# One layer of a hybrid token mixer: a mask moved behind a product, a scaling moved to ScalarE, larger VectorE instructions, and a new written-out order

## The chip, the cores and the metric

The kernel runs on one core of one Trainium2 chip. The metric is the device time of one execution in microseconds, here the median of three runs. All work is float32; large products run as three products of two float32r halves.

## The reference

The function is one layer over 512 latent tokens and 256 context tokens, width 1024. What matters here is its first half:

```python
zc = _modulate(_rmsnorm(hc, g_pre1), csh1, csc1) @ w_in     # context, 7584 columns
z  = _modulate(_rmsnorm(h,  g_pre1), sh1,  sc1)  @ w_in     # latent
# RWKV-7 branch, 16 heads of 64, two directions:
def step(s, inp):
    r_t, w_t, k_t, v_t, kk_t, b_t = inp
    s_a = einsum('dbhvk,dbhk->dbhv', s, -kk_t)
    s = s * w_t[..., None, :] + s_a[..., None] * b_t[..., None, :] + v_t[..., None] * k_t[..., None, :]
    return s, einsum('dbhvk,dbhk->dbhv', s, r_t)
# RG-LRU branch: gates, then h = a * h + b over the tokens, two directions
mixed = gates[..., :D] * (y_a @ w_branch_a) + gates[..., D:] * (y_b @ w_branch_b)
h = h + gt1 * _rmsnorm(mixed @ w_out, g_post1)
# then a mixture of 64 experts (top 6) with a shared expert, and a last residual
```

The modulation vectors come from `silu(c) @ w_mod + b_mod`.

## The kernel before

The kernel has three parts in time. First the tokens are normalized, and the first third of the modulation is computed. Then `mixers()` (line 548) runs the input projection and both mixers. Then `moe()` runs the output projection, the router and the experts. The change touches `mixers()` alone, besides one constant.

The mixers work on eight pairs of heads (j, 128 channels each). A pair has three stages g of 256 tokens: one of context and two of latent tokens, so there are 24 stages n = 3j + g. A stage holds both directions d, and in each four chunks i of 64 tokens. The sequential recurrence is turned into products per chunk:

- `s1` (1011) makes the decay and its running product; `s1c` (1049) makes from it the operands AR (key and receptance, scaled) and BK (three slots of 64 columns per chunk; slots 0 and 2 hold the same product k times the inverse decay, slot 0 for the lower and slot 2 for the upper 64 partitions, slot 1 the second key).
- `s1b` (1109, "A-stage") multiplies BK with AR into PSUM and masks the result to its causal half, into AM. Stage 0 of a pair has one such product group, stages 1 and 2 have two. It then transposes BK into BKt.
- `p_sub` (1233) inverts the 16x16 diagonal blocks: AM goes to a DRAM buffer Dg, comes back as L with one block per partition, DVE substitutes, and the result goes back through Qg. In line 1248 POOL then sets AM's entries inside the diagonal blocks to zero, in place, by the constant `offd`.
- `p_mrg` (1298) merges the 16x16 inverses into a 64x64 one: a first product of AM with the block diagonal DD, copied by ACT into NT, and three more steps (`mm`, then an addition on DVE).
- `p_chain` (1341) runs over the chunks. Per chunk: a first product of the state H and of AM with UV into `ch`; a copy X on DVE; a product with Q; copies into UV on DVE (one half) and ACT (the other); a product with BKt; and the new state H = Pc * (product) + HP on DVE, where HP = H * Pc is the old state scaled by the decay Pc, made by POOL (1381). In stages 1 and 2 the output products into `py` follow.

Beside these run `p_in` (675, the input projection, 128 columns at a time, in steps of two of its eight row blocks), `weight_stream` (483, loads a weight half, splits it on ACT and DVE), `p_lru` (746), `p_uv`, `p_kk`, `p_bonus`, `p_post` (1458, the normalization after a pair's chain), `p_br` (859, the branch projections) and `p_mod` (903: the other two thirds of the modulation, 16 rounds of a 1 MB load and 8 products; at its end it stores zeros into the two buffers `y_d` that the experts add into, with sixteen DMAs on SyncE's queue). `p_mod` borrows the buffers of `y` and `kds`, so that stage 1 (n = 1) of `s1c` and of the chain starts after it.

Each of these fifteen is a generator. Between two `yield`s it issues the instructions of one step, mostly for one engine. `Flow.run` (137) walks through the string ORDER: each letter with its number advances one generator so many steps. As PE, DVE, ACT and POOL keep the order in which instructions are issued, this string alone sets each engine's queue. SyncE's DMAs are placed by the same program order. A generator may also yield an event or a lock (PSUM buffers `a` and `b` are shared through locks); these too take one advance.

The instruction on the end of the loop reads:

```python
yield ACT if first else DVE
if first: S.activation(Hn[:, d, :], ch[:, 4 + d, :], AF.Copy, scale=Pc[:, d, i:i + 1])
else:     V.scalar_tensor_tensor(Hn[:, d, :], ch[:, 4 + d, :], Pc[:, d, i:i + 1], HP[:, d, :], op0=ALU.mult, op1=ALU.add)
```

Of the kernel before, what the change touches and what calls it, by code (L numbers as in the profile page):

```python
# [63 lines left out]
PE, DVE, ACT, POOL = "PE", "DVE", "ACT", "POOL"  # L64
ORDER = (
    "idwi2ludri4w2idniwi6ciwsw2iei2widiwiwi3wiwiwi3w2i2wiwi2bwi2ldwi5w3idw2miriwi2ri3r2w2ir2driwrwkwiwiriroirik2i5rik"
    "wldrwi3w3ri2kwkilpkikiluwuilil2irkiwuliulwiliukdwkurlukiuwlire2wie2wieiwei2u2ruiwreuwe2uediwdudweirie2ie2l2idib"
# [3 lines left out]
    "b3r2b4erlb2e2r2se2bererseserebe3s4crs4es6res5e3relb2ibi2rkbir2sbmblwrmwr2lrmklr2mrli2lrlb2mlwnlbimibrnibimlbmrsi"
    "mkmc2b2csrlckckeirc3wi2wkrc2kcscwi2kcs2ws2rsws2rcs2r2s2c2s3c2sciricksrc2kscncsc2skirscinsewcec3ic3wemierme3iwcie"
    "cewc2eicrne2cem2emc2ecmeliliwlmr2wcbcumlimlucwkl3ulmcb2mcuriucwcrb2cbucibc3wscblic3licecicwciebier2eis2ececiece3"
    "bcscw2scs2r2cswurscis4rc2sircs4cscucisc2irsi2cicscsc2iecrwicwc2isce2ciu2eremumu3meucpiewirwup2eiemepwerbwmlrcibl"
    "rl3ml3pmlipl2pb2primbieibrbwmerirwmwmrpcpc2bceieb2wc2bpribwecesic3e2cwilcpeiwiwbeicepcspiwcprecp2crcs3rs4c2sps3c"
    "scs3iwpscisbcsw2c3eicsciwrsc2se2crwcsc3meu2iure2u2e2iuwi2b2ibr2lbkbcrmblir2kr2lcwl2mlriwirl2umb2mnlmlwbmbim2uri"
    "b2rimkmwc2sli2skecnwcbcwbkcricsirc2srsisis3kcri2ckcs5csnskrw2rkcwc2ics3rc2kcsrc2s2crickc2nwsec2sic2icie2c2ece2nw"
    "emecicmiwe3cieceicm2ec2rmcmwcmeimewlulwlumlbiu2lclrwlburlmblbci2mbc2rcb2cuwc2l2urbwukecrc3ecbecic2eciceberece2i"
    "e2s2ri4sc3ec2eswrsrwcscirs2csiscrcws2rs3cs2i2scscsicw2csics2crcsc2mcieiewrc5u2reiuipiru2eurmeieuiurprwpm2e2relbr"
    "lrwrmwlipl2miblprpilbwcblwl3miwemimiebcibm2c2b2ecb2cbibwiececpecp2ececes2ipbcirsepwcew2cwiciricwpec2bpcrcipscs6"  # L80
    "c3ls4pscsipse2sc2swcpsecwpcsic2sicwic2rpecescesrceu2wic2uiu2ebmwrurbwmrbi2bri2bmlbuklwr2irnrlurlwmrl2nilrbrlbmlb"
    "lbkmsibikwisi2m3wb2mrmc5bkisc3srwr2ckcscki2si2sws2csls2icsrsckcrkscscsrkiswscsrcec2kwnwc2scsikec3ensc3wcicrc2e2c"
    "semecie2kciw2mieci2ecmece2cec3memwremui2blmlrwumlrclir2wml2wmnbl2ulirmubrl2c2wec2b2ceuibubc2ecsbcre2cbecscic2ic"
    "i2ci2uececbe2wr2sc3i2e2srs3c3srus2cscrscsecwics3iw2csrisc2scrsc3wscesic3i2ci2cscicueusueuimuepucuweiwue2r2iermr2"
    "eimwpwpilwrlmbmplpr2lrbl2rmpilmli2mblbwicmrlwrib3lmewmec2ecbibecwibpb2cwpcecpeieblpeiceisec2eic2prwc2espwiwcse2c"
    "iwcsc2p2sp2s4c2peps4rs2pcrs2csiwscsc2icisciwes2cwcbwc3sc2e2ci2e2umurmnu2w2ubibrkiuilbr2nurmbkibwmbrwrlwlrl2r2l2u"
    "licrbr2imbrkbmlmlibmbw2biscs2imilmbmcwc3kbkicrciekcrcicrc2is4is2rsiskskw2s2c2rc2sirs2c2sckicnwrscscskc3rscs2ikei"
    "c3ieie4wmcmc2nce2rwe2icic2ec2ecwkie2cmimewc3memlwcicmlcmurlcrblmlrl3bnwirblmumiuc2lblrcbcb2cbwceuce2cir2ecece2uc"
    "eciuwcscic2i2bcieieresecwrbcsecs3ic2rcis2w2crcs2ucsus2icswscsrs2c2siscircsrwsc2ic5ec2sc2uei2rirusuiumueueweiepru"
    "iui2pewrewem2iwbwpmrpbml3mrlml2pr2l2ir2iblpcriribwb3wimibml2we2mbmcec2iwbc2bcscsbe2cipc2epwe2cwi2pcicip2ecespewc"  # L90
    "ecwpc2picricwsps2bscesps2crplpscs5piscs2ircscwc2bwicseisc2wsercicecsc3u3cieuwmue2uelrb2rw2biri2burnbirm2wbilrmwr"
    "lml4ur2krwbl2imb2mbirsrmlbklbikcnmisrmswmwcebwbrc2kci2c3i2crcki2k2c2r2iwscws3ns5csrcscrs3icscksicsrcrkc2kcs3cwi"
    "c2wkeic2nwesikwcecmcicrime2c2iece2rec4iceie3iecwcre2lm2cmc2lmlmblcblrnwlrlurwmbuluiumrmlcmuc3buic2b2clclbcswirw"
    "c3eciec2ibe2i2ecsebicerciwuecsceicbwcere2cwes2rcs2crics2ic2swur2cs2isis3wiscicscscsrisc3scs2cic2meceic3iuruwu2c"
    "u2perermieie2ieu2mwcp2ebrl2iwmrwirmwl2rml3mliwb2rpml3iwebmibp2ibrimbwebmc2ebecbircsbrbpcecpipcwe3src2eipewci2wps"
    "ewc2ecwpcicibcwprc2sipscs3p2csr2pes4pcscs2ilspc2ws2wcswci2csc2s2iec2ecrcse2c2ecuwu2beiumuieiulbnbrmbwrbr2cib2lri"
    "niur2umwrlmlilrmrlrl3wbicmbwkiwrkblblwbmsmbwiwimib2km2c2sc2rckic2rcskr2kci2cs2ikisciscrws2csickes2rcrskcsic2scsi"
    "ks3rsc2wcisrcwsnwcrskc3nsec2i2ec3erecewiecic2e3cecm2ewimcirc2wem2ec2m2eicwe2l2c2bmlr2l2mulinwl2b2ilmlkmwbucwcurb"
    "ucurcbuc2rici2cisbcliebcbecesrceciwescibc2ie2ieuce2wecec2weusrsrsc4rs4cs2crscis3csi2wcs2cscisicrcsrwc5ecs2c2i3e"
    "c2uwmu2ewurueueimimiuipruepewe2prpl2prwliwcbrlprpm2lrlbplmibr2il2rwbpmbrmicilblb2mibimwb2sepewpewribe2wmc2pecewp"  # L100
    "sceceiecpsepe2bces4cisicwcs2rc2ps2iepsps3wscwr2isc2isc2iscpwilwcscsiwscrcsbciecrwceic2icoecec2oemwlkcrkc2bokokrc"
    "k3lrcmcoblmrlu2l2o2lu3bol2ubnbmobo2momncub2mulbobm2bskloem2bnwocsob2cock2cocokcncsce3osc4s2ecoc3scscs2c3scos2csc"
    "ososcs2o2co2escscwscocseo2s2c3ewewewc2oe2ocmo2ncececec2wc2me2l3cw2uwmlml2ouob2lmlcwbmbl2umb2lme2cemomsueoemc2bec"
    "wbe4o2webcucscswocecueceuc2wus3cecsowoes2wc2soc2se3scs2c3ocscsoswcwc2oswsc3oscs2cebwowcoseocesmlmwbwc3l2col4clc2"
    "lc2wco2lbmcwubo2lebu2mu2bwbmobwm2wb2mbeomcem2sc2b2epec3eo2e2ceu2cesucscpoecpcecwcwp2cwop2cs3cp2cebseco2pcwscpws"
# [2212 lines left out]
```

## Time and profile before

| | |
|---|---|
| time, median of 3 runs | 2006.52 us (2000.51 to 2008.1) |
| the profiled execution | 2014.62 us, its span 2012.7 us |
| mean granted TensorE clock | 0.936 |
| PE busy | 1741.5 us (87%) |
| DVE busy | 1095.7 us (54%) |
| ACT busy | 714.3 us (35%) |
| POOL busy | 553.9 us (28%) |
| HBM read, written | 340.72 MB, 56.92 MB |

PE is TensorE's products, DVE is VectorE, ACT is ScalarE, POOL is GpSimd, SP or SPq is SyncE and its queue of DMAs. A line L1248 is line 1248 of the kernel. Times in the rows are microseconds from the start of the span. An engine's idle time is put down to what ended it. The granted clock is a share of TensorE's full 2.4 GHz. The mixers run from about 55 to about 1232 us.

### The profile page before, as it was taken

What the parts mean: (1) busy time and instruction counts of PE and PEld (TensorE: products, weight loads), DVE (VectorE), ACT (ScalarE), POOL (GpSimd) and SP (SyncE); (2) the same over time, 40 slices, a digit from 0 to 9 for tenths busy, and PEclk for the clock granted to TensorE, in tenths of its full rate; (3) what the DMA queues carried; (4) which work ended last, traced back from release to release, by engine and by line L of the source; (5) the groups of instructions that cost most, each with busy time, mean ns of one, the idle gap of its engine ahead of it and who ended that gap; (6) DMA issues with size and microseconds to landing.
All of it is one profiled execution on the core that took longest, in us unless ns stands there. A gap on an engine that the chain in (4) does not pass through costs nothing.

```text
span 2012.7 us, 41091 instructions
## 1 busy us (share of the span) xinstructions
PE 1741.5 (87%) x16550; PEld 1106.0 (55%) x16550; DVE 1095.7 (54%) x2721; ACT 714.3 (35%) x1308; POOL 553.9 (28%) x557
## 2 busy tenths in 40 slices
...
GB/s 278 155 140 158 142 112 59 68 84 56 87 58 73 78 64 82 58 87 63 77 123 114 106 155 250 288 210 303 387 372 306 347 376 387 320 379 396 405 353 130
DMA packets 310267, 386.72 MB, mean 192 GB/s; under 512 B 172390, under 2 KB 252860, under 8 KB 292540
## 3 DMA queue, kind: packets, MB, share of 16 engines
...
HBM read 340.72 MB, written 56.92 MB: 198 GB/s over the span
## 4 chain that ended last, share of the span: by engine, by line
PE 59%; DMA 14%; DVE 13%; issue 7%; ACT 5%; SPq 1%; POOL 1%; DVEq 0%; POOLq 0%; ACTq 0%
PE ps_zl L524 17%; PE mgu L2187 10%; PE my L1690 5%; PE ps_m L1321 4%; PE ps_zc L526 3%; DMA wgu<-in_ex_w_gu 2%; DMA y_d<-ys,ix 2%; DMA DD<-Qg 2%; DMA ug<-u_d,ix 2%; PE ps_a L774 2%; PE ps_a L1126 2%; DMA wdn<-in_ex_w_down 2%; PE ps_z L1572 1%; PE ps_c L1400 1%; PE pt L2180 1%
## 5 line engine op out<-in xcount | busy, mean ns | idle before, releaser
L2187 PE MATMUL mgu<-wgu,uTe 128*32 128x512 f32 (+2 forms) x1488 | 310.8, 614 | 23.5 <-DMA wgu<-in_ex_w_gu 18.4
L524 PE MATMUL ps_zl<-xh,wh 128*128 128x512 f32 (+1 forms) x600 | 267.7, 446 | 6.7 <-DVE xh L452 2.6
L524 PE MATMUL ps_zl<-xl,wh 128*128 128x512 f32 (+1 forms) x600 | 243.2, 405 | 2.7 <-DVE xl L453 1.7
L524 PE MATMUL ps_zl<-xh,wl 128*128 128x512 f32 (+1 forms) x600 | 242.3, 404 | 0.8 <-DVE wl L505 0.8
L2187 PEld LDWEIGHTS mgu<-wgu,uTe 128*32 128x32 f32 (+2 forms) x1488 | 92.1, 129 | 193.6 <-issue 162.0
L2195 POOL DMA_INDIRECT y_d<-ys,ix x65 | 93.3, 1436 | 257.3 <-DVE ys L1693 208.1
L505 DVE TENSOR_TENSOR wl<-wraw,wh 128x512 fp32r<-128x512 f32 (+1 forms) x152 | 112.2, 738 | 83.0 <-ACT wh L502 62.5
L1690 PE MATMUL my<-wdn,hT 128*32 128x512 f32 (+2 forms) x776 | 153.4, 603 | 1.9 <-ACT hT L1686 1.4
L524 PEld LDWEIGHTS ps_zl<-xh,wh 128*128 128x128 f32 (+1 forms) x600 | 114.8, 191 | 51.9 <-issue 10.1
L524 PEld LDWEIGHTS ps_zl<-xh,wl 128*128 128x128 f32 (+1 forms) x600 | 115.6, 193 | 30.7 <-DVE wl L505 2.1
L524 PEld LDWEIGHTS ps_zl<-xl,wh 128*128 128x128 f32 (+1 forms) x600 | 116.3, 194 | 26.7 <-DVE xl L453 3.4
L1381 POOL TENSOR_TENSOR HP<-H,Pc 128x128 f32<-128x128 f32 x88 | 55.2, 627 | 262.8 <-DVE H L1409 210.5
L1693 DVE COPY ys<-my 128x512 f32<-128x512 f32 x41 | 28.3, 691 | 181.3 <-ACT ys L1692 175.4
L502 ACT ACTIVATE wh<-wraw 128x512 fp32r<-128x512 f32 (+1 forms) x152 | 94.6, 622 | 84.3 <-PE ps_zc L526 25.4
L1668 DVE SCALAR_TENSOR_TENSOR th<-th,mgu 128x256 f32<-128x256 f32 x39 | 16.0, 415 | 174.4 <-ACT th L1667 174.4
L1667 ACT ACTIVATE th<-mgu 128x256 f32<-128x256 f32 x39 | 14.7, 383 | 270.2 <-PE mgu L2187 262.1
L1248 POOL TENSOR_TENSOR AM<-AM,offd 64x512 f32<-64x512 f32 x48 | 71.1, 1481 | 115.3 <-DMA Dg<-AM 104.7
...
L1690 PEld LDWEIGHTS my<-wdn,hT 128*32 128x32 f32 (+2 forms) x776 | 49.8, 129 | 90.7 <-issue 72.2
L2180 PE MATMUL pt<-ident,ug 128*128 128x128 f32 x296 | 51.6, 307 | 51.3 <-DMA wdn<-in_ex_w_down 25.4
L1692 ACT ACTIVATE ys<-my 128x512 f32<-128x512 f32 x41 | 24.5, 597 | 179.1 <-PE my L1690 172.2
L1394 ACT ACTIVATE UV<-ps_c 64x128 f32<-64x128 f32 x96 | 25.7, 267 | 163.5 <-DVE UV L1391 163.1
(505 smaller groups left out, 3733.3 us busy)
## 6 DMA issues: line engine op xcount, KB each, us to landing
...
wraw<-in_w_in SPq DMA_DIRECT2D x118, 256.0 KB
...
```

Source lines behind the costliest of these rows:

```text
L502: S.activation(wh[:, :, 0:n], raws[m][:, :, 0:n], AF.Copy)
L505: V.tensor_sub(wl[:, :, 0:n], raws[m][:, :, 0:n], wh[:, :, 0:n])
L524: T.matmul(zl[:n], w[:, kc % 4, 0:n], x[:, kc, LAT], start=a, stop=z)
L526: T.matmul(zc[:n], w[:, kc % 4, 0:n], x[:, kc, 0:CTX], start=a, stop=z)
L774: T.matmul(o, gw[q, 2 * d + g, :], r, start=True, stop=True, tile_position=(64 * h, 64 * h))
L1248: G.tensor_tensor(AM[q, h, :, :, 0:64], AM[q, h, :, :, 0:64], offd[q, None, None, :].to_broadcast([64, 4, 2, 64]), op=ALU.mult)
L1321: T.matmul(pm[q, m, 0:w], lhs(q, m), rhs(q, m), start=True, stop=True, tile_position=(64 * h, 64 * h))
L1381: G.tensor_tensor(HP, H, Pc[:, :, i:i + 1].to_broadcast([128, 2, 64]), op=ALU.mult)
L1690: T.matmul(py[q, hf, :], hT[:, k, q], wd[:, k, 512 * hf:512 * hf + 512], start=k == 0, stop=k == 1, tile_position=(0, q.start))
L2180: T.transpose(pt[:, k, :], ug[:, k:D:KC], ident)
L2187: T.matmul(gu[q], uT[:, k, q], wg[:, k, :], start=k == 0, stop=k == KC - 1, tile_position=(0, q.start))
L2195: G.indirect_dma_start(out=y[:, :], out_offset=bass.IndirectOffsetOnAxis(ap=ix[0:n], axis=0), in_=ys[q, :], in_offset=None, bounds_check=S ...
```

## The change

Five things change, all inside the mixers.

The constant `offd` was 1 where the column lies in a later block of 16 than the row, for AM; it becomes 1 where the row lies in a later block than the column, for the product, whose rows are AM's columns:

```diff
-        V.tensor_tensor(offd, cb, pm, op=ALU.is_gt)
+        V.tensor_scalar(cb, cb, 16.0, None, op0=ALU.add)
+        V.tensor_tensor(offd, pm, cb, op=ALU.is_ge)
```

`p_sub` no longer masks AM on POOL, and `p_mrg` masks the first product as it copies it:

```diff
-                for h in range(2):
-                    q = slice(64 - 64 * h, 128 - 64 * h)
-                    yield POOL
-                    lab(f'relayout:{n//3}.{n%3}')
-                    G.tensor_tensor(AM[q, h, :, :, 0:64], AM[q, h, :, :, 0:64], offd[q, None, None, :].to_broadcast([64, 4, 2, 64]), op=ALU.mult)
...
-                yield ACT
-                L()
-                S.activation(NT[:, :, 0:48], pm, AF.Copy)
+                yield DVE
+                L()
+                V.tensor_tensor(NT[:, :, 0:48], pm, offd[:, None, 0:48].to_broadcast([128, 8, 48]), op=ALU.mult)
```

The scaled state HP is made by ScalarE, one instruction for each direction:

```diff
                     if not first:
-                        yield POOL
-                        L()
                         HP = r2.tile([128, 2, 64], F32, name="HP", bufs=1)
-                        G.tensor_tensor(HP, H, Pc[:, :, i:i + 1].to_broadcast([128, 2, 64]), op=ALU.mult)
+                        for d in range(2):
+                            yield ACT
+                            L()
+                            S.activation(HP[:, d, :], H[:, d, :], AF.Copy, scale=Pc[:, d, i:i + 1])
```

Slots 0 and 2 of BK are written for both directions, all chunks and all partitions by one instruction after the loop over d, and the causal mask of A is applied to both heads by one instruction:

```diff
-                yield DVE
-                L('lora+elem')
-                V.tensor_tensor(BK[0:64, d, :, 0, :], c3(kd[0:64]), c3(Ei[0:64, d, :]), op=ALU.mult)
-                yield DVE
-                L('lora+elem')
-                V.tensor_tensor(BK[64:128, d, :, 2, :], c3(kd[64:128]), c3(Ei[64:128, d, :]), op=ALU.mult)
...
+            yield DVE
+            L('lora+elem')
+            c4 = lambda t: t.rearrange("p d (i t) -> p (d i) t", t=64)[:, :, None, :].to_broadcast([128, 8, 2, 64])
+            V.tensor_tensor(BK.rearrange("p d i s t -> p (d i) s t")[:, :, 0:3:2, :], c4(tha), c4(Ei), op=ALU.mult)
...
-                for h in range(2):
-                    yield DVE
-                    L('A-stage')
-                    V.tensor_tensor(AM[:, h, i0:i0 + per].rearrange("p i d w -> p (i d) w"),
-                                    pa[:, h].rearrange("p i d w -> p (i d) w"),
-                                    mask[:, None, 0:W].to_broadcast([128, per * 2, W]), op=ALU.mult)
+                yield DVE
+                L('A-stage')
+                V.tensor_tensor(AM[:, :, i0:i0 + per].rearrange("p h i d w -> p h (i d) w"),
+                                pa.rearrange("p h i d w -> p h (i d) w"),
+                                mask[:, None, None, 0:W].to_broadcast([128, 2, per * 2, W]), op=ALU.mult)
```

ORDER is a new string throughout: 5000 advances in place of 5072. The letters are c chain, m `p_mrg`, u `p_uv`, b `p_s1b`, s `p_sub`, e `p_s1c`, l `p_s1`, k `p_kk`, r `p_lru`, o `p_br`, d `p_mod`, n `p_bonus`, p `p_post`, i `p_in`, w the weight stream. Its first and its last line:

```diff
-    "idwi2ludri4w2idniwi6ciwsw2iei2widiwiwi3wiwiwi3w2i2wiwi2bwi2ldwi5w3idw2miriwi2ri3r2w2ir2driwrwkwiwiriroirik2i5rik"
...
-    "w2o2p2wowo2pwow2opop2wop2owpwpwpop"
+    "pwlcibormdi3dwidi2ni2dui3w4i4wiwi2wedwi2kwi5wi3w3idi2w2i2sw2i4diw2iwi2widirw2i4r4w2rwidri2r2irliwiwrir2di2k2rkld"
...
+    "cw2owco2c2wc3o2wcwcwoc2o2woc4ocwcwc2wc2o2c2wc3o2cwc2oc2ocop3wp2op2wp3w2p3owp2opop2owp2w2p2o"
```

## Rows read from the trace of the kernel before

**Rows 1.** Windows: busy us and count of each engine, clock, DMA share, GB/s.
```profile
60.00:240.00 180.00, 169.93 (x1249) 118.33 (x1249) 80.58 (x135) 80.59 (x148) 20.12 (x19) 0.97 0.52 151
240.00:295.00 55.00, 29.02 (x161) 20.61 (x159) 43.88 (x69) 23.15 (x33) 22.59 (x21) 0.66 0.42 129
...
60.00:1240.00 1180.00, 1065.42 (x12951) 804.47 (x12952) 831.91 (x1735) 573.78 (x1031) 360.80 (x377) 0.95 0.38 99
```

**Rows 2.** Waits of PE, 60 to 1240 us: total us, times, longest.
```profile
PE ps_c L1400 <- ACT UV L1394: 26.8, 31, 2.8
PE ps_c L1387 <- DVE X L1376: 18.8, 26, 2.6
...
PE ps_a L1126 <- DVE BK L1093: 11.0, 2, 7.2
PE ps_c L1370 <- DVE H L1409: 10.2, 21, 1.9
```

**Rows 3.** Timelines of SP, DVE, POOL, 242 to 296 us: start, us, engine, line, operation.
```profile
246.83 10.21 SPq L958 DMA_DIRECT2D y_d<-mw  x16
...
274.97 1.50 DVE L1093 TENSOR_TENSOR BK<-tha,cum 64x256 f32<-64x256 f32 x1
276.50 3.47 DVE L1096 TENSOR_TENSOR BK<-tha,cum 64x256 f32<-64x256 f32 x1
...
272.11 3.99 POOL L1248 TENSOR_TENSOR AM<-AM,offd 64x512 f32<-64x512 f32 x2
```

**Rows 4.** Two lines by themselves: durations in ns, least, median, longest.
```profile
L1096 DVE TENSOR_TENSOR BK<-tha,cum x48: 422/423/3469, 133.4 to 1136.8; 64x256 f32<-64x256 f32 x48
...
L1409 DVE SCALAR_TENSOR_TENSOR H<-ps_c,Pc,HP x176: 265/278/289, 200.5 to 1212.6; 128x64 f32<-128x64 f32 x176
```

**Rows 5.** Groups by line and shape: busy us, mean ns, idle us before and its releasers.
```profile
L1248 POOL TENSOR_TENSOR AM<-AM,offd 64x512 f32<-64x512 f32 x48 | 71.1, 1481 | 115.3 <-DMA Dg<-AM 104.7 <-DVE AR L1079 7.4 <-DVE hq L883 1.2
L1381 POOL TENSOR_TENSOR HP<-H,Pc 128x128 f32<-128x128 f32 x88 | 55.2, 627 | 262.8 <-DVE H L1409 210.5 <-DVE QL L1251 18.7 <-ACT H L1407 14.7
...
L1329 ACT ACTIVATE NT<-ps_m 128x384 f32<-128x384 f32 x24 | 11.8, 491 | 41.1 <-PE ps_m L1321 41.1
...
L1394 ACT ACTIVATE UV<-ps_c 64x128 f32<-64x128 f32 x96 | 25.7, 267 | 163.5 <-DVE UV L1391 163.1
...
L1407 ACT ACTIVATE H<-ps_c,Pc 128x64 f32<-128x64 f32 x16 | 4.1, 310 | 2.5 <-PE ps_c L1400 2.5
...
L1136 DVE TENSOR_TENSOR AM<-ps_a,mask 128x512 f32<-128x512 f32 x80 | 52.2, 683 | 16.2 <-PE ps_a L1126 13.3 <-PE ps_a L1130 2.9
...
L1096 DVE TENSOR_TENSOR BK<-tha,cum 64x256 f32<-64x256 f32 x48 | 25.2, 525 | 1.0
L1093 DVE TENSOR_TENSOR BK<-tha,cum 64x256 f32<-64x256 f32 x48 | 23.5, 490 | 0.1
L1057 DVE SCALAR_TENSOR_TENSOR aE<-tha,cum 128x512 f32<-128x512 f32 x24 | 19.6, 815 | 0.5 <-ACT cum L1046 0.2
L1337 DVE TENSOR_TENSOR Qf<-ps_m,DD 128x384 f32<-128x384 f32 x24 | 13.2, 552 | 31.3 <-PE ps_m L1321 31.3
```

**Rows 6.** Groups by line: the loads of ScalarE's function table, mixers.
```profile
L788 ACT ACT_TABLE_LOAD x16 | 20.5, 1283 | 0.3
...
L715 ACT ACT_TABLE_LOAD x1 | 1.3, 1283 | 0.0
```

**Rows 7.** The chain that ended last, 50 to 64 us: start, us, what.
```profile
55.87 2.96 DMA mw<-in_w_mod
...
58.96 3.56 PE ps_y L923 x8
```

**Rows 8.** The loads of tile mw, as in rows 4.
```profile
L915 SPq DMA_DIRECT2D mw<-in_w_mod x64: 327/382/1400, 55.9 to 230.8; - x64
```

**Rows 9.** Timeline of PE, 1205 to 1262 us, as in rows 3.
```profile
1215.48 1.02 PE L1474 MATMUL ps_b<-y,bones 128*128 128x512 f32 x2
...
1230.28 1.02 PE L1524 MATMUL ps_b<-gdT,lg 128*128 128x512 f32 x2
```

More of the change, by code (lines that the diff above doesn't have):

```diff
@@ L71 @@
[L71 to L105, printed above, removed]
@@ new lines @@
+    "k2d2riwrkirirkwlrdi2rwi2diwirdil3ilwiluli2wkw2rkwuik2l2ulewide2ier3e2r2erwuireiuiuwreieiruier4dewrbib3iwib2iwlwr"
+    "wisuwirirbdwbrsulilcsisirlsuir2s2l2i3slsi2swlcs3i2sdlsw2is2isiwis2ulwiwisi2di2mwluiwmwri2wmr2iwmwr2dmrur3mwirir2"
+    "mwimur2emwd2r2dir2d3imd2c2e2iwce3reciewec3riec2re3we2ce2c2wcricewcbr2icrcbrwbc2brirb2w3bcb2i2cicicbribc2i3clc3l2"
+    "crciciclwrslil2crlrwrlicr2ciwlscisc2wku2lrweci2swsuies2esres2wieuerie3sieulwes3w2sisruisise2w2i2urirseieisebnbni"
+    "busrbwrnbrkmnknwiwbikikriblcm2kbmbwkbkir3kwib2mkmksrirwkm2i3mrmlc4ls3ls2l2c3slilcsilc2wslcs3leceicswese2scwese3"
@@ new lines @@
+    "c2icwecwsi2wsic2icsiwc2s2ececisweielc2mclcmlmil2c3wlc4l3wicbimirwc3mcirclwcle2mercmc2rmc2b2murubmcbumieb2seuewr2"
+    "e2uc2wrcuc2wec2ec2re3ib2eurirececiecewrc2il2clrcs2c2wilwirsiclrirlcls2clilbl2cwsc2ie2rscs5cwis2c3siscswusecw2i2s"
+    "ic2wir2cr2icsc3rsci2kcmcrcric3r2ic2icwmirbcbmur2brwirimipwbelibmcwbmwuiwb2mibe2msrbrerubime2uewewe2rumwemrcicrc"
+    "e2ceikcrn2kis2ws2cswil2clc2iswscsls2lbs2c2i2luilcsic2ulclirus2nicnincikcw2lkwcsklckc2srpkrcpkpep2ikc2srs2pk2cper"
+    "cpieprwscp2mcwiripcprpc2icpr2mcpmpwpc3i2cbmumeb2mb2mcebimibuci2b2ebrmerer2me2mcec4e2icewlsubcblwciwlc2il4cscls6c"
@@ new lines @@
+    "iulsuwls2lcescs2ce2wsicecicesuicsi2cswcscwcic4iscsc2sciuw3ic2mcwci2riwrcmcmcic2wrcwcwrmcuc2mcrmrbueiurmb4cmiube2"
+    "meuersre2bcumbmce2cierc3iececerwcuwicewl2iliulc3r3cucsc2ilslslrlsc2icl2srs3rswclseiswswc2siecbsc2s2iecscw2iscri2"
+    "cwcisrcrc2rcs2cicricicrc3ici2c2wrc2rcrmbubrwmibrmbierwmubi2wbwumwi2bmrsrmirbkmbebciwerue2bwlrmemereireruewmc4ec"
+    "e2iceniknsrwscs2kpws2cslc2lws2is2lcbuc3ilci3scul2slcliruilicnlninkcs2lskcw2kcsrpkeckpkc3ispicpwrc2rsckps2mk2erp2"
+    "ep2cprirwpwcpc4pwcmpipmpcipcir2impc2b2eibmemrurub2umibr2bumi2bimbre2mecemcec2secec2be2ic2blbwcilwlclwc2ics2ls3lc"
@@ new lines @@
+    "s2l3sc2sclsiwuclwi2es3cics2uc2sic2e2secsc2icwicsciwcwisuecsmcwc4i2micic2wcrwmuwcimcwrcmwcr2cwcrcmcr2b2eimbmibms"
+    "b2u2ere3u2e2becmuecmc2ecier2crecwicwciecuwcecblilcirl2crl2cliclslrc2s3clciurs2lc2weswresicws2cs4isesc4ruirswc2w"
+    "i2sicrcsrwcrcicscscirc3icirmcbic2kc3ircricr2mb2mbw2b2irumibpuermwmuilw2r2wb2rbibm2irece2rersibre2mi2ecwewmuerewm"
+    "cec2ecen2riukbi2cscsks3cslw2siwscls2cslcilc2lcuiclcsil2i2usuinsic2sln2ilkwkcsilckwr2ckwkcpc2ksrpckricepskscp2ks"
+    "p2cripwp2rc2spewcerpc3pmcirimp2mcp2c2rmiewprcicbuibmrb2cbrumrmibicimbrbseiubme5m2c3icbeceiwbce2lulwclc3lcws2ls2l"
```

28 lines of the change are left out of this document (21 added, 7 removed).

## The prediction

> **What bounds the kernel now.** I read first the windows that cut the span by stage. From 60 to 1240 us run the token mixers, the only part the change touches. There PE is busy 1065 of 1180 us, DVE 832, ACT 574, POOL 361 [rows 1]: TensorE is the bound, and what can be won is its 115 us of idle time and the time at half clock. The granted clock averages 0.95 of 2.4 GHz; with two levels (2.4 and 1.2 GHz) that is 2 x 0.05 x 1180 = 118 us at 1.2 GHz. The matrix products are the same in both versions, so the change cannot shorten PE's work, only its waits.
>
> Next come the waits of PE in that stretch [rows 2]. Three belong to the loop of the chain, in which each 64-token chunk passes PE four times with a copy on DVE or ACT between: 26.8 us for the ScalarE copy of UV, 18.8 us for X, 10.2 us for the state H, 55.8 in all. 11.0 us are two waits for BK. The window 240 to 295 us holds one clump: PE idle 55 - 29.0 = 26.0 us at a mean clock of 0.66 [rows 1].
>
> Last, the timeline inside that clump [rows 3]. SyncE spends 10.2 us issuing the sixteen zero stores that end `p_mod`, then DVE makes BK slowly: one instruction takes 1.50 us and the next 3.47 us, while POOL runs the merge mask for 3.99 us. The median of the second line is 0.42 us [rows 4]. So POOL's mask does not only occupy POOL: it stretches DVE.
>
> **The change part by part.** Sums are made against the profiled execution (2014.62 us: span 2012.7 and 1.9 around it), 8.1 us above the median 2006.52; I carry the difference over to the median.
>
> *Mask moved.* 48 POOL instructions at 1.481 us go, 71.1 us, and with them 104.7 us in which POOL's queue stood waiting for the DMA that reads AM [rows 5]. In their place the copy of the first product into NT leaves ACT (24 x 0.491 = 11.8 us) and becomes a DVE multiply of 128x384 from PSUM, like the first form of L1337: 24 x 0.552 = 13.2 us [rows 5].
>
> *State scaling.* 88 POOL instructions, 55.2 us, become 176 on ACT. Nearest rows: 0.267 us (L1394) and 0.310 us (L1407), so 47 to 55 us [rows 5]; I take 47.5. Each waits for H, and the ACT queue is in order: behind it stand the UV copy of the same chunk, weight splits and evacuations of the input projection. POOL stood 210.5 us in that wait, 42 times [rows 5].
>
> *Larger instructions.* 96 BK instructions (23.5 + 25.2 = 48.7 us) become 24 of 128x1024. One 128x512 with two SBUF operands takes 0.815 us (L1057); a 1024 lies between that and twice it, I take 1.3: 31 us, 18 less. 80 masks of A at 0.683 become 40 of double size: between 27 and 55 us, I take 1.21 us each, 48, 4 less than 52.2 [rows 5]. DVE therefore changes by -18 - 4 + 13 = -9 us, plus what POOL's 126 us no longer stretch: of the BK time, 25.2 - 48 x 0.423 = 4.9 us of L1096 alone lie above its median [rows 4].
>
> The SBUF page of the Trainium skill ("SBUF — State Buffer", Who interferes with whom) has one port pair shared by VectorE and GpSimd as an exclusive lock for a whole instruction, against VectorE work with two SBUF inputs. The trace agrees: 3.47 us against 0.42 beside POOL, while the H update, with one input in PSUM, is never over 0.289 us [rows 4]. By the rule a BK instruction four times as long can also wait, or make POOL wait, for one long stretch; at 24 x 4 us (the longest POOL piece here) it would take back up to 96 us of DVE time, most of it not on PE's path.
>
> *Order: the stall after p_mod.* I wrote out both strings with the generators' yields; each gives 971 steps on PE. Before, 3 PE steps stand between the last step of `p_mod` and the first A-stage step of stage 1, and 3 between that and the first A-stage step of stage 2: nothing covers DVE's work. After, it is 11 and 24. The whole stall is worth 26.0 us idle, plus the half clock: 2 x 0.34 x 55 = 37 us, half of the 53% of it in which PE was busy, 10 us. Bounds: 36 us won, or nothing if it only moves. I take -26, because the zero stores still hold SyncE for 10 us with weight loads behind them.
>
> *Order: the chain.* Of 96 chunks, the step from the Q product to the BKt product has no other PE step between in 17 before and 5 after, and on average 0.94 then 1.21; from there to the next chunk 2 then 0 without, 1.53 then 1.86 (72 pairs). The step waiting for X is unchanged (20 and 19). So the waits of 26.8 and 10.2 us shrink and 18.8 stays; half of 37 would be 18. Against it, the ACT instructions queued between the start of a chunk and its UV copy go from 1.65 to 4.82, of which the scalings are 1.83. I take -12; bounds -37 (both vanish) to +27 (the first doubles).
>
> *ScalarE's function tables.* Counting switches between the sqrt and the tanh/exp functions in ACT's order gives 62 before (the trace shows 61 loads in the mixers, on eight lines of which the first and the last stand in [rows 6], 1.283 us each) and 46 after: -16 x 1.283 = -20.5 us. ACT thus changes by +47.5 - 11.8 - 20.5 = +15 us: 49% to 50% busy. The page "ScalarE: Activation LUTs" of the Trainium skill (What ACT_TABLE_LOAD costs) puts a drain on top, 2.66 us a switch, by which ACT would end at -7; the rows show at most 0.3 us of idle before sixteen of these loads together, so I keep 1.283.
>
> *Half clock elsewhere, DVE's relief.* 118 - 37 = 81 us at half clock outside the stall cost at most 0.9 x 81 / 2 = 36 us; a sixth of it for the waits that go: -6 (bounds 0 to -20).
>
> *p_mod earlier.* Its 16 rounds of PE work spread over 112 steps before, 74 after. Before, a round came every 10.8 us (first and last load 55.9 and 230.8 us [rows 8]), a 1 MB load and its products took 2.96 + 3.56 us on the chain [rows 7]; two thirds of 10.8 is 7.2, hardly more than 6.5, and weights queue on SyncE beside it. DMA must rise from 151 GB/s [rows 1] by 46. I take +5; bounds 0 and 16 x 1.3 = 20.
>
> *The tail.* Between the first and the last product of the last `p_post` PE has ten input-projection steps now (1215.48 to 1230.28 us [rows 9]), three after; at (14.8 - 2.6) / 10 = 1.2 us each that is 8.5 us of cover less for a chain of small steps on DVE, ACT and POOL. I take +3, bounds 0 and 8.5.
>
> Sum: -26 - 12 - 6 + 5 + 3 = -36. That is 1978.6 for a profiled execution, and 2006.5 - 36 = 1970.5 for the median.
>
> **Rivals.** *The stall only moves.* The new order is as fixed as the old one, and the old one has its clump where DVE slowed beyond what its place in the order allowed; the new one has 1.3 us BK instructions beside POOL's long ones, and earlier `p_mod` rounds. For it: those surprises are not visible in the strings. Against it: cover rises nearly everywhere. With the chain unchanged and 10 us of a new stall: 2006.5 - 26 + 5 + 3 + 10 = 1998.5.
>
> *ScalarE becomes the chain's bound.* If the two scalings of a chunk end after DVE's half of the UV copy, every chunk waits for them: 88 x 0.54 = 47.5 us on PE's path, no gain in the chain: 2006.5 - 26 - 6 + 5 + 3 + 47.5 = 2030. It decides from the point where ACT reaches the scaling late, behind a 1 us function or a table load. For it: the queue before the UV copy triples in number; POOL's 210.5 us of waiting now falls to a working engine. Against it: ACT is half idle, H is ready before the chunk's first product starts, and ACT already stood 163.1 us waiting at that copy [rows 5].
>
> *Much better.* If half of all idle time goes (57 us) and half of the cost of the half clock (18 + 5), it is 2006.5 - 80 = 1926.
>
> **Numbers.** Forecast 1970.5 (own range 1950 to 1990) 0.52; much better 0.15; stall moves 0.20, of which 0.08 ends faster and 0.12 same; ScalarE bound 0.13, of which 0.02 ends same. Half a per cent, 10 us, is about what a measurement can tell from no change. Faster 0.75, same 0.14, slower 0.11. The range 1928 to 2008 leaves out the ScalarE rival and the best of the better case, some 0.17.
>
> **What would show it.** Right: in the windows, PE idle between 150 and 300 us below 20 us and no stretch at a mean clock near 0.66; `p_mod`'s last load near 180 us instead of 230; the wait for the UV copy below 20 us in total; no POOL row for the mask or HP; DVE some 20 us lower, ACT table loads near 46. Wrong: PE's idle in the mixers still near 115 us, waits for the scaling on ACT, or waits for `mw` of over 1 us each in the first 100 us. If the mixers end where they did, only the stall moved.

## The result, and the profile after

The kernel after takes 1949.42 us (median of 4 runs, 1944.5 to 1969.72) against 2004.34 us: a ratio of 0.9742, interval 0.9698 to 0.9787. That is 55 us less, 21 us more than forecast. Its profiled execution took 1946.59 us, with a span of 1943.7 us, at a mean clock of 0.957 (0.936 before).

The first product of the branch projection on `xh`, at the end of the mixers, marks where the change ends. By the tile `xh` (least/median/longest ns, then first and last start) it begins at 1233.9 us before and at 1180.4 us after, 53.5 us earlier:

```profile
L1598 PE MATMUL ps_pl<-xh,wh x4: 389/441/795, 1233.9 to 1257.6; 128*128 128x512 f32 x4
```
```profile
L1593 PE MATMUL ps_pl<-xh,wh x4: 389/441/569, 1180.4 to 1204.3; 128*128 128x512 f32 x4
```

What follows, unchanged code, took 778.8 us in the profile of before and 763.3 in that of after. This is not the change: in the fourteen profiles of this study it takes 763 to 767 us in six kernels and 775 to 779 in eight (among these runs 8 and 11, the kernel after with two and five advances moved), and the profile of before (2014.62 us) lies 10 us above the median. So causes are read below from the mixers, and times from the medians.

Windows of the kernel after (columns as in [rows 1]):

```profile
60.00:240.00 180.00, 159.94 (x1226) 106.74 (x1225) 92.18 (x169) 84.79 (x159) 26.54 (x27) 0.96 0.56 166
150.00:300.00 150.00, 135.49 (x1506) 99.39 (x1502) 103.75 (x207) 75.93 (x151) 35.34 (x35) 0.97 0.48 131
240.00:295.00 55.00, 52.30 (x767) 42.09 (x767) 42.93 (x82) 29.58 (x61) 12.88 (x12) 1.00 0.33 76
...
60.00:1180.40 1120.40, 1042.14 (x12967) 786.97 (x12965) 777.82 (x1644) 584.55 (x1172) 230.02 (x239) 0.98 0.40 102
```

The clump of [rows 1] is gone: 26.0 us of PE idle at clock 0.66 became 2.7 at 1.00. From 60 us to the mixers' end PE is idle 78.3 us; in the kernel before, by the same window up to 1233.9 us, 112.1:

```profile
60.00:1233.90 1173.90, 1061.82 (x12944) 802.28 (x12944) 828.99 (x1731) 571.86 (x1030) 356.86 (x375) 0.95 0.38 98
```

So the 53.5 us are 33.8 us of idle time and 19.7 us of PE busy time, at 23 products more. The busy time is the clock: at two levels (full and half) a mean of 0.95 over 1173.9 us is, as an estimate, some 117 us at half clock, and 0.98 over 1120.4 us some 45. The waits of PE, 60 to 1240 us, against [rows 2]:

```profile
PE ps_m L1314 <- DVE Qf L1331: 11.6, 5, 3.2
PE ps_c L1382 <- DVE X L1370: 11.2, 22, 1.1
PE ps_c L1395 <- ACT UV L1389: 10.2, 17, 1.6
PE ps_a L1148 <- DVE AM L1134: 6.8, 6, 2.3
...
PE ps_m L1314 <- DVE NT L1323: 5.3, 6, 1.2
PE ps_c L1364 <- DVE H L1404: 4.0, 9, 0.7
```

The chain's three waits fell from 55.8 to 25.4 us. The merge's wait for Qf is now the largest. The groups that answer to [rows 5]:

```profile
L1376 ACT ACTIVATE HP<-H,Pc 128x64 f32<-128x64 f32 x176 | 55.0, 344 | 26.8 <-DVE H L1404 23.2 <-POOL xc L899 2.8 <-DVE ltmp L1263 0.6
L1134 DVE TENSOR_TENSOR AM<-ps_a,mask 128x1024 f32<-128x1024 f32 x40 | 48.7, 1217 | 5.7 <-PE ps_a L1125 4.8 <-PE ps_a L1129 0.4
...
L1103 DVE TENSOR_TENSOR BK<-tha,cum 128x1024 f32<-128x1024 f32 x24 | 29.3, 1222 | 0.2
...
L1323 DVE TENSOR_TENSOR NT<-ps_m,offd 128x384 f32<-128x384 f32 x24 | 13.2, 551 | 13.2 <-PE ps_m L1314 13.2
```

`p_mod` ends at 191 instead of 231 us (its loads, against [rows 8]), and PE now stands at its first product:

```profile
L915 SPq DMA_DIRECT2D mw<-in_w_mod x64: 327/382/1541, 55.1 to 191.2; - x64
```
```profile
58.17 4.32 PE L923 MATMUL ps_y<-mw,cTw 128*32 128x512 f32 x8 [7.56 <-DMA mw<-in_w_mod]
```

### The profile page after: what moved, and what is told of

It reads as the page before. It is cut to its first block, busy times and chain, and to the rows that moved or that the text cites. A ratio compares the mean times of both kernels' runs of the same rounds, so it can differ in the third digit from the quotient of the medians.

```text
span 1943.7 us, 40959 instructions
## 1 busy us (share of the span) xinstructions
PE 1703.9 (88%) x16550; PEld 1079.3 (56%) x16550; DVE 1046.9 (54%) x2634; ACT 724.7 (37%) x1444; POOL 427.3 (22%) x421
## 4 chain that ended last, share of the span: by engine, by line
PE 58%; DVE 12%; DMA 11%; ACT 8%; issue 8%; SPq 1%; POOL 1%; ACTq 0%; POOLq 0%; DVEq 0%
PE ps_zl L524 15%; PE mgu L2182 13%; PE my L1685 6%; PE ps_m L1314 3%; PE ps_zc L526 2%; DMA wdn<-in_ex_w_down 2%; DMA y_d<-ys,ix 2%; PE pt L2175 2%; PE ps_z L1567 1%; DMA ug<-u_d,ix 1%; PE ps_a L1125 1%; DVE wl L505 1%; PE ps_c L1395 1%; PE ps_a L1025 1%; DMA t<-lg_d 1%
## 5 line engine op out<-in xcount | busy, mean ns | idle before, releaser
L2182 PE MATMUL mgu<-wgu,uTe 128*32 128x512 f32 (+2 forms) x1488 | 307.0, 611 | 20.8 <-DMA wgu<-in_ex_w_gu 15.7
L505 DVE TENSOR_TENSOR wl<-wraw,wh 128x512 fp32r<-128x512 f32 (+1 forms) x152 | 116.3, 766 | 55.6 <-ACT wh L502 54.3
L524 PEld LDWEIGHTS ps_zl<-xh,wl 128*128 128x128 f32 (+1 forms) x600 | 113.9, 190 | 30.4 <-DVE wl L505 2.6
L1307 POOL TENSOR_SCALAR Qf<-DD 128x128 f32<-128x128 f32 x24 | 16.1, 671 | 409.3 <-DMA DD<-Qg 409.3
L1791 POOL DMA_INDIRECT ug<-u_d,ix x37 | 38.8, 1048 | 217.3 <-PE mhT L1679 88.2
L2175 PEld LDWEIGHTS pt<-ident,ug 128*128 128x128 f32 x296 | 39.5, 196 | 70.4 <-issue 64.8
L1404 DVE SCALAR_TENSOR_TENSOR H<-ps_c,Pc,HP 128x64 f32<-128x64 f32 x176 | 43.3, 277 | 49.7 <-PE ps_c L1395 34.1
```

Of the source, the lines that this page charges most:

```text
L505: V.tensor_sub(wl[:, :, 0:n], raws[m][:, :, 0:n], wh[:, :, 0:n])
L524: T.matmul(zl[:n], w[:, kc % 4, 0:n], x[:, kc, LAT], start=a, stop=z)
L1791: G.indirect_dma_start(out=ug, out_offset=None, in_=u_d[:, :], in_offset=bass.IndirectOffsetOnAxis(ap=ix[:, 0:1], axis=0), bounds_check=SE ...
L2175: T.transpose(pt[:, k, :], ug[:, k:D:KC], ident)
L2182: T.matmul(gu[q], uT[:, k, q], wg[:, k, :], start=k == 0, stop=k == KC - 1, tile_position=(0, q.start))
```

## The experiments

Theory A: the new order made the gain. Theory B: the instructions made it, since POOL no longer stretches VectorE. In the table "end" is the first branch product on `xh`, "idle" and "busy" are PE's from 60 us to there. Every ratio is to runs of the kernel before that were made beside it.

| kernel | median us | ratio | end | idle | busy |
|---|---|---|---|---|---|
| before | 2004.3 | | 1233.9 | 112.1 | 1061.8 |
| after | 1949.4 | 0.974 [0.970, 0.979] | 1180.4 | 78.3 | 1042.1 |
| 1 new instructions, old order | 1987.8 | 0.994 [0.991, 0.997] | 1217.7 | 99.1 | 1058.6 |
| 2 old instructions, new order | 1999.6 | 0.998 [0.995, 1.002] | 1232.5 | 114.5 | 1058.0 |
| 3 HP on POOL | 1951.1 | 0.975 [0.969, 0.982] | 1180.6 | 73.5 | 1047.1 |
| 4 mask on POOL | 1989.7 | 0.995 [0.993, 0.998] | 1214.5 | 103.5 | 1051.1 |
| 5 NT on ACT, no mask | 1968.6 | 0.982 [0.977, 0.986] | 1197.6 | 82.6 | 1055.0 |
| 6 spare POOL product | 1979.9 | 0.988 [0.985, 0.992] | 1210.1 | 94.0 | 1056.1 |
| 7 order and mask alone | 1981.5 | 0.990 [0.985, 0.994] | 1200.1 | 89.7 | 1050.4 |
| 8 first p_mod step later | 1959.6 | 0.977 [0.971, 0.983] | 1184.2 | 77.8 | 1046.4 |
| 9 spare POOL, one operand | 1965.1 | 0.981 [0.976, 0.986] | 1194.5 | 84.2 | 1050.4 |
| 10 BK small | 1966.1 | 0.982 [0.978, 0.987] | 1196.6 | 88.7 | 1047.9 |
| 11 merge addition first | 1957.1 | 0.976 [0.972, 0.980] | 1182.3 | 73.9 | 1048.4 |
| 12 RG-LRU steps later | 1939.2 | 0.970 [0.966, 0.973] | 1167.4 | 71.5 | 1035.9 |

Each end comes from one profile. The code ahead of the mixers is the same everywhere, yet the first product on `xh` starts between 42.4 us (the kernel after) and 45.9 us (run 8); so ends within some 3 us of each other are not told apart. The times of runs 1, 4, 7, 8, 9, 10 and 11 lie outside every range that had been written for them, by 1.5 to 9.7 us.

**1 and 2: each half alone.** Run 1 has all edits of the change but ORDER, run 2 the new ORDER with none of the others.

```diff
 # run 1: the code of after, ORDER of before, advances dropped or added where their forerunners stood
-    "pwlcibormdi3dwidi2ni2dui3w4i4wiwi2wedwi2kwi5wi3w3idi2w2i2sw2i4diw2iwi2widirw2i4r4w2rwidri2r2irliwiwrir2di2k2rkld"
+    "idwi2ludri4w2idniwi6ciwsw2iei2widiwiwi3wiwiwi3w2i2wiwi2bwi2ldwi5w3idw2miriwi2ri3r2w2ir2driwrwkwiwiriroirik2i5rik"
...
 # run 2: the code of before, ORDER of after, the old advances put back (the mask just before QL)
```

> All four instruction changes (mask after the product, state scaling on ScalarE, one BK instruction, one A mask instruction for both heads), but the advances in the order of the kernel before; only the advances that no longer exist are dropped, and those that are new stand where their forerunners stood. Theory A (the order made the gain): the clump after p_mod stays, because three PE steps still stand where DVE needs some ten us; 1990 to 2002 us, a gain of 3 to 14 of the 55, and PE idle in the mixers above 95 us. Theory B (the instructions made it: POOL's mask and scaling no longer stretch DVE and no longer hold up what is queued behind them): 1955 to 1970 us, PE idle in the mixers below 85 us, the window 240 to 295 us at a clock above 0.85. If both are half right, some 1975 us.

> The instructions of the kernel before in the new order; the dropped advances are put back beside their successors (mask on POOL just before the product that reads AM, HP on POOL). Theory A: 1952 to 1965 us, no clump after p_mod, PE idle in the mixers some 85 to 95 us. Theory B: 1985 to 2000 us, with POOL's mask again beside BK instructions of several us and PE waiting for BK or AM.

Alone the order is worth 1.4 us at the mixers' end and the instructions 16.2; together they are worth 53.5. Neither theory holds. In run 1 the clump stays (window 240 to 295 us, then waits of PE):

```profile
240.00:295.00 55.00, 29.54 (x190) 21.04 (x183) 38.67 (x63) 25.61 (x38) 22.26 (x20) 0.66 0.43 130
```
```profile
PE ps_c L1395 <- ACT UV L1389: 25.4, 27, 3.2
PE ps_a L1125 <- DVE BK L1103: 14.1, 2, 13.4
PE ps_c L1382 <- DVE X L1370: 13.2, 26, 1.5
```

In run 2 the clump goes:

```profile
240.00:295.00 55.00, 52.08 (x672) 41.18 (x670) 45.82 (x92) 28.85 (x54) 16.61 (x16) 1.00 0.33 73
```

ACT's first UV copy of stage 2 comes at 303.8 us, against 344.2 before. The gain is then lost bit by bit. From that copy to the one of stage 20 run 2 takes 759.1 us, the kernel before 736.6 (for 82 products fewer, among them 24 of each kind of the input projection, as an estimate some 8 us), the kernel after 716.9. The windows between these copies, of before, after and run 2:

```profile
344.20:1080.80 736.60, 674.61 (x9168) 520.42 (x9169) 580.60 (x1235) 395.61 (x713) 259.42 (x274) 0.97 0.32 77
```
```profile
298.30:1015.20 716.90, 673.37 (x9250) 518.51 (x9248) 547.47 (x1179) 412.49 (x828) 149.47 (x165) 0.99 0.32 77
```
```profile
303.80:1062.90 759.10, 684.83 (x9250) 528.62 (x9248) 590.43 (x1247) 387.93 (x713) 242.88 (x267) 0.97 0.31 73
```

PE does the same 9250 products in the last two. It is idle 43.5 us with the new instructions and 74.3 with the old. Run 2 waits for the chain as before, and for NT on ScalarE:

```profile
PE ps_c L1399 <- ACT UV L1393: 25.6, 30, 2.6
PE ps_c L1386 <- DVE X L1375: 19.1, 30, 1.4
PE ps_m L1320 <- ACT NT L1328: 16.0, 4, 5.2
...
PE ps_c L1369 <- DVE H L1408: 7.3, 15, 1.7
```

The time lies in theory B's range, but theory B's sign is missing: the longest BK instruction took 1.52 us, not several. The order's greater cover in the chain, by itself, took 3.8 us off the chain's 55.8. A limit of runs 2 and 4: the advances were put back by one rule, so they show this order with these instructions, not the best order for them.

**3 and 4: one instruction change undone in the new order.**

```diff
 # run 3
-    S.activation(HP[:, d, :], H[:, d, :], AF.Copy, scale=Pc[:, d, i:i + 1])
+    G.tensor_tensor(HP, H, Pc[:, :, i:i + 1].to_broadcast([128, 2, 64]), op=ALU.mult)
 # run 4, with offd as in the kernel before
+    G.tensor_tensor(AM[q, h, :, :, 0:64], AM[q, h, :, :, 0:64], offd[q, None, None, :].to_broadcast([64, 4, 2, 64]), op=ALU.mult)
...
-    V.tensor_tensor(NT[:, :, 0:48], pm, offd[:, None, 0:48].to_broadcast([128, 8, 48]), op=ALU.mult)
+    S.activation(NT[:, :, 0:48], pm, AF.Copy)
```

> The kernel after with only the state scaling HP put back on POOL, one instruction for both directions. Theory A: 1947 to 1957 us, ACT some 55 us less busy, the wait for the UV copy unchanged or smaller. Theory B: POOL's scaling waits for the state and stretches DVE beside it, so 1960 to 1975 us and DVE busy up by over 8 us. A third reading, that ScalarE's 176 scalings stand before UV copies and cost the chain: 1930 to 1945 us, faster than the kernel after.

> The kernel after with only the merge mask put back: POOL sets AM's entries in place before the Q transposition, ACT copies the first product of the merge without a mask. Theory A: 1947 to 1957 us. Theory B: the mask takes 71 us of POOL and stretches DVE beside it, so 1960 to 1980 us, DVE busy up by more than 10 us although it loses the 13 us of the masked copy, and single BK or A-stage instructions of over 2.5 us.

The state scaling is worth nothing: 0.2 us at the mixers' end. The mask is worth 34.1 us, against theory A; the time, 1989.7 us, lies above theory B's range too. DVE is busy 1076.2 us over the execution, 29.3 more than in the kernel after, though NT's 13.2 us have left it. Run 4's wait and its POOL group:

```profile
PE ps_m L1318 <- ACT NT L1326: 15.3, 4, 5.1
```
```profile
L1245 POOL TENSOR_TENSOR AM<-AM,offd 64x512 f32<-64x512 f32 x48 | 77.1, 1607 | 39.4 <-DMA Dg<-AM 21.4 <-DVE wl L504 11.0 <-DVE tha L1086 3.9
```

**5 and 6: the mask's two sides apart.** Run 5 has the old copy and leaves the mask out altogether, run 6 has POOL's products without the old copy. Run 6's products work on the upper half of a tile whose lower half is DVE's `ltmp`, so not quite on a tile of their own; in its trace no other engine waits for them.

```diff
 # run 5
-    V.tensor_tensor(NT[:, :, 0:48], pm, offd[:, None, 0:48].to_broadcast([128, 8, 48]), op=ALU.mult)
+    S.activation(NT[:, :, 0:48], pm, AF.Copy)
 # run 6, twice a stage at the old mask's places; spare is half of a [128, 512] tile
+    G.tensor_tensor(spare, spare, offd[64:128, None, :].to_broadcast([64, 8, 64]), op=ALU.mult)
```

> The kernel after with ScalarE copying the first merge product into NT, and no mask anywhere: the mask is left out of the computation. In the same order. It takes from the run with the mask on POOL its POOL instructions and keeps its copy on ScalarE. Theory P (POOL's 48 long products stretch DVE, and that is what the mask on POOL costs in the new order): 1940 to 1955 us, like the kernel after, DVE some 13 us less busy. Theory Q (the copy into NT on ScalarE comes behind other work of that queue, and PE waits for it, 15.3 us in four waits with the mask on POOL): 1962 to 1985 us, with PE's wait for NT of ACT again near 15 us.

> The kernel after, NT masked on DVE as there, and beside it 48 POOL products of the old mask's shape (64x512, two SBUF operands, in place) at the places of the old mask, on a tile of their own: they wait for nothing and nobody waits for them. Theory P (stretch alone): DVE busier by 25 to 45 us and 1965 to 1990 us. Theory Q (queue and dependence): 1945 to 1957 us, DVE busy up by less than 10 us.

Both sides cost, 17.2 and 29.7 us at the mixers' end; together (run 4) 34.1, so they overlap. Run 5 shows how PE comes to wait 3.2 to 5.0 us, four times, for a copy of 0.48 us: ScalarE stands for a DMA of the RG-LRU, and NT is queued behind it (timeline of ACT at the first place, the waits of PE, windows).

```profile
413.98 0.63 ACT L828 ACTIVATE lq<-t 128x512 f32<-128x512 f32 x1 [4.59 <-DMA t<-lg_d]
...
415.52 0.48 ACT L1323 ACTIVATE NT<-ps_m 128x384 f32<-128x384 f32 x1
```
```profile
PE ps_m L1314 <- ACT NT L1323: 16.4, 4, 5.0
```
```profile
410.00:415.00 5.00, 1.11 (x28) 0.85 (x24) 0.83 (x3) 0.99 (x2) 4.34 (x5) 0.84 0.50 147
415.00:420.00 5.00, 3.94 (x106) 3.94 (x108) 1.50 (x4) 1.78 (x5) 0.00 (x0) 0.50 0.01 3
```

In the window after the wait the clock is 0.50, all of it at half (the kernel after has 0.69 there, behind its wait of 3.2 us for Qf). In the 10 us behind the other three waits it is 0.55, 0.84 and 0.55; at the same places the kernel after, behind shorter waits, has 1.00, 1.00 and 0.83. Of run 5's 17.2 us only 4.3 are idle time; 12.9 are busy time for the same products. In run 6 DVE is busy 1076.1 us over the execution instead of 1046.9, though nothing waits for the spare products, and the 24 BK instructions take 37.4 instead of 29.3 us:

```profile
L1106 DVE TENSOR_TENSOR BK<-tha,cum 128x1024 f32<-128x1024 f32 x24 | 37.4, 1558 | 0.2
```
```profile
L1248 POOL TENSOR_TENSOR both<-both,offd 64x512 f32<-64x512 f32 x48 | 79.1, 1648 | 3.8
```

**7 and 10: the larger instructions undone.** Run 7 has HP on POOL and BK and the A mask in small pieces, with the order and the moved mask; run 10 only BK small.

```diff
-    V.tensor_tensor(BK.rearrange("p d i s t -> p (d i) s t")[:, :, 0:3:2, :], c4(tha), c4(Ei), op=ALU.mult)
+    V.tensor_tensor(BK[0:64, d, :, 0, :], c3(kd[0:64]), c3(Ei[0:64, d, :]), op=ALU.mult)
+    V.tensor_tensor(BK[64:128, d, :, 2, :], c3(kd[64:128]), c3(Ei[64:128, d, :]), op=ALU.mult)
```

> The new order and the moved mask alone: HP on POOL, BK in pieces of 64x256 and the A mask by head as before. If order and mask together make the gain: 1945 to 1960 us. If the larger VectorE instructions are a part of it (DVE some 20 us busier by their fixed costs): 1965 to 1980 us.

> The kernel after with only BK put back into four pieces of 64x256 for each stage (96 instead of 24 instructions; the A mask stays one instruction for both heads). DVE should be some 22 us busier by the two rows (51.5 against 29.3 us). If that occupation is what the new order does not bear, most of the loss of the run with order and mask alone comes back: 1968 to 1982 us. If the loss lay in the A mask by head or in the two together: 1948 to 1960 us.

Run 7 ends its mixers 19.7 us later than the kernel after; the rest of its 32 us lies behind them, where this profile took 776.0 us against 763.3. BK alone costs 16.2 of the 19.7 us. Its groups in run 10 add up to 50.8 us, against 29.3 in one instruction a stage, and the chain pays:

```profile
L1093 DVE TENSOR_TENSOR BK<-tha,cum 64x256 f32<-64x256 f32 x48 | 27.4, 571 | 0.0
L1096 DVE TENSOR_TENSOR BK<-tha,cum 64x256 f32<-64x256 f32 x48 | 23.4, 488 | 0.7
```
```profile
PE ps_c L1396 <- ACT UV L1390: 15.2, 26, 1.6
PE ps_c L1383 <- DVE X L1371: 13.3, 21, 1.1
```

21.5 us more of DVE work cost 16.2 us of the kernel's time, on an engine that is 69% busy there (778 of 1120 us). What is left, some 3 us, is too little to tell; the A mask was not tried alone. In the new order the parts add up: the mask's 34.1 us (run 4) and these 19.7 make 53.8, and all undone together (run 2) cost 52.1.

**9: a POOL instruction with one operand.**

```diff
 # run 6's spare product becomes
+    G.tensor_scalar(spare, spare, 1.0, None, op0=ALU.mult)
```

> As the run with 48 spare POOL products, but each spare instruction is a TENSOR_SCALAR with one SBUF operand, 64x512 in place, at the same places. If it is POOL's two-operand products that stretch DVE: DVE busy within 8 us of the kernel after and 1945 to 1957 us, although POOL is some 60 us busier. If any POOL work on SBUF of that length does it: DVE busier by 20 us or more and 1968 to 1985 us, as with the product.

In between: DVE is busy 1057.1 us (10 more, not 29), the end is 14.1 us later, not 29.7 (2.1 of the 14.1 lie ahead of the mixers). It takes POOL as long as the product:

```profile
L1248 POOL TENSOR_SCALAR both<-both 64x512 f32<-64x512 f32 x48 | 80.9, 1685 | 4.0
```

Where the 14 us come from, beyond 5.9 of idle and 8.2 of busy time of PE, stays open.

**8: p_mod's first steps later.**

```diff
-    "pwlcibormdi3dwidi2ni2dui3w4i4wiwi2wedwi2kwi5...
+    "pwlcibormdi3dwi3ni2dui3dw4i4wiwi2wedwi2kwi5...
```

> The kernel after with the first product step of p_mod moved four input-projection advances later and the second three, as late as in the kernel before. If the 7.6 us in which PE stands for the first mw load, and the half clock behind it, are lost time: 1936 to 1943 us, PE waiting for mw under 1 us. If the load is only the first thing to be late (the input projection's own operands come next): 1946 to 1953 us.

The wait for `mw` fell from 7.6 to 2.1 us. This profile starts its mixers 3.5 us later than that of the kernel after; counted from their start, stage 2 began 6.2 us earlier, but the mixers ended 0.3 us later. The time, 1959.6 us, is not told apart from that of the kernel after. So taking the wait away won nothing by the mixers' end; where the 6.2 us went stays open.

**11 and 12: the wait that is left.** The wait for Qf comes in five pairs, at the place where run 5 lost: DVE's addition stands behind an RG-LRU step, which stands behind ScalarE's DMA. Run 11 moves the addition, run 12 the six last RG-LRU advances (by 16 to 29 places; the expectation says 24 to 31).

```diff
 # a piece of ORDER at stage 5: after, run 11, run 12
-    cwrmcuc2mcrmrbueiurmb4cmiube2
+    cwrmcuc2mcrm2rbueiurb4cmiube2
+    cwmcuc2mcmbueiumb4cmiube2mreu
```

> The kernel after with five advances moved: in stages 5, 8, 11, 14 and 17 the first addition of the merge stands on DVE directly behind its product, no longer behind an RG-LRU step that itself waits for ScalarE. If the 11.6 us that PE waits there for Qf are lost time: 1938 to 1944 us, the wait below 3 us. If the next wait takes its place (the chain's, or the weights'): 1945 to 1953 us.

> The kernel after with the six last RG-LRU advances of five pairs (from the ScalarE Square that waits some 4.6 us for its DMA, to the last product on DVE) moved 24 to 31 advances later on average, behind the second addition of the merge of stages 5, 8, 11, 14 and 17. If the order of ScalarE's and DVE's queues at that place costs PE its 11.6 us of waits for Qf, and a shorter stay at half clock behind each: 1930 to 1942 us, the wait for Qf below 3 us, the mixers' first branch product on xh at 1164 to 1172 us instead of 1180.4. If the ScalarE instruction only holds up other work there (the copies of UV, BKt): 1945 to 1955 us.

Run 11 moved the addition too little, and its time lies above both of its ranges: the first RG-LRU step on DVE (L831) still stands before it, after 3.82 us for ScalarE.

```profile
412.06 0.43 DVE L831 TENSOR_SCALAR lq<-lq 128x512 f32<-128x512 f32 x1 [3.82 <-ACT lq L828]
412.41 0.55 DVE L1331 TENSOR_TENSOR Qf<-ps_m,DD 128x384 f32<-128x384 f32 x1
```
```profile
PE ps_m L1314 <- DVE Qf L1331: 8.9, 5, 2.8
```

Run 12 took it out. The wait for Qf is 0.5 us, and the mixers end 13.0 us earlier than in the kernel after. Of these, 2.8 us were there at stage 2 already, ahead of the first moved advance, so about 10 are the edit's. From 188.7 to 994.0 us its mean clock is 1.00. The window 408 to 420 us, in the kernel after and in run 12, shows PE busy 8.82 and 10.84 of 12 us, at clock 0.86 and 1.00 (the work in it is not quite the same):

```profile
408.00:420.00 12.00, 8.82 (x211) 7.43 (x208) 6.48 (x13) 3.91 (x10) 5.24 (x7) 0.86 0.31 93
```
```profile
408.00:420.00 12.00, 10.84 (x175) 8.69 (x174) 10.86 (x27) 8.50 (x19) 2.71 (x3) 1.00 0.40 107
```
```profile
PE ps_m L1314 <- DVE Qf L1331: 0.5, 2, 0.3
```

With a median of 1939.2 us (6 runs, 1932.2 to 1954.5) run 12 is the fastest of all: 10 us below the kernel after. The two ratios' intervals overlap slightly, but the trace shows where about 10 us went.

## Why the prediction was right, and where it was not

The forecast of 1970.5 us had the sign and the places right. The likeliest case was 21 us too high; the time lies just below its own range of 1950 to 1990. The sum adds order and instructions as if each stood alone: the order's terms come to -30 us and the instructions' to -6, where each alone gave -1.4 and -16.2 us at the mixers' end (runs 2 and 1). That the whole came out near is in part luck.

- **The stall (-26) with p_mod earlier (+5).** The clump went, by the order, as said (it stays in run 1 and goes in run 2): PE idle from 150 to 300 us is 14.5 us, under the 20 that was named. The windows from 60 us to the UV copy of stage 2, before and after:

```profile
60.00:344.20 284.20, 245.40 (x2137) 175.24 (x2137) 160.45 (x285) 131.57 (x230) 52.47 (x54) 0.90 0.45 130
```
```profile
60.00:298.30 238.30, 215.24 (x2057) 151.43 (x2056) 137.99 (x257) 116.02 (x223) 39.66 (x40) 0.97 0.50 144
```

  PE's idle time fell from 38.8 to 23.1 us and its busy time by 30.2, in part as work moved to later: of the input projection 68 products of 128x512 fewer (480 and 412, tile `ps_zl`) and 12 of 128x256 (216 and 204, `ps_zc`). At full clock they follow each other every 0.23 and 0.12 us, so I estimate 17 us. So some 29 of the 45.9 us were won, 15.7 of idle time and 13 of clock (0.90 before, 0.97 after); 12 more of each kind, some 4 us, had slipped past 60 us, where PE had stood 7.6 us for `mw`. The net is 25 us, against 21 said. I had priced half clock in the clump alone, not over this whole stretch. The +5 is not shown: run 8 took the new wait for `mw` away and won nothing by the end. The reading behind the +5 was off too: the rounds came every 11.6 us (first loads of the first and last round 55.9 and 229.4), not 10.8, and come every 9.0 now, not 7.2.

  POOL's mask did not make the clump: in run 1 it is gone, and PE waits up to 13.4 us for BK. The 3.99 us in [rows 3] are two instructions; the longest single one in the kernel before took 2.62, and at 24 times that the 96 us said of BK would be 63:

```profile
L1248 POOL TENSOR_TENSOR AM<-AM,offd x48: 1260/1282/2617, 148.1 to 1149.6; 64x512 f32<-64x512 f32 x48
```

- **The chain (-12).** This step failed in its reason. The waits fell by 30.4 us, but not by the cover that I counted in the two strings: with the order alone they fell by 3.8 (run 2), with the instructions alone to 42.6 us (run 1). Counting steps of PE between a product and its copy did not tell what the copy itself stands behind in its queue. The fall needed both halves of the change.
- **Half clock elsewhere and DVE's relief (-6).** Undersized. From the UV copy of stage 2 to the mixers' end the time fell by 7.6 us while 80 and 24 products of the input projection came in, some 21 us by the same estimate: about 28 us won, where the chain, this term and the tail together had 15. I costed 9 us less DVE work, and the end of POOL's stretch, as almost free on an engine off PE's path. In the new order BK's 21.5 us are worth 16.2 us (run 10) and POOL's 48 products 29.7 us (run 6). DVE fell by 48.8 us, 1095.7 to 1046.9, where I had named 20. PE's idle time there fell by 18.1 us: the chain's 30 us less were given back in part by the merge, whose wait for Qf rose from 1.2 to 11.6 us, which no step of the sum had.
- **The tail (+3).** From the UV copy of stage 20 to the mixers' end PE was idle 11.3 us before and 11.7 after: nothing.
- **Prices.** BK 1.222 us (1.3 said; the longest 1.32, so none was held up for long), A mask 1.217 (1.21), NT 0.551 (0.552). HP 0.344 us each, 55.0 in all, the upper bound, not the 47.5 taken. Table loads in the mixers 61 to 45 (46 said), and the next instruction starts 12 ns behind a load in the median, which bears out 1.283 us a load; ACT rose 10.4 us (15 said).
- **Rivals.** ScalarE did not become the chain's bound: run 3 shows HP worth 0.2 us either way. That the stall would only move was true of run 2, the order without the instructions, 1999.6 us, where that rival had 1998.5, though the loss was spread over 18 stages and not in one new stall.
